# Up-products of a gated MLP with the activations stationary instead of the weights, in three parts of the hidden width

## The chip, the cores and the metric

The kernel runs on one core of one Trainium2 chip. The metric is the time of one execution on the device in microseconds (us); the median of several runs is given, and one further execution was recorded by the hardware profiler. The engines are named as the profile names them: PE is TensorE's matrix multiplication and PEld its loading of the stationary operand, DVE is VectorE, ACT is ScalarE, POOL is GpSimd, and SP issues the transfers.

## The reference

Two encoder layers work on 256 tokens of width 2048, in float32. Layer 0 mixes tokens with a bidirectional mLSTM, layer 1 with a bidirectional HGRN2 recurrence; each mixer is followed by a gated MLP with a convolution of width 3 over the tokens, and a final RMSNorm closes the trunk. The change touches the MLP, whose hidden width is 5504 (43 tiles of 128, called f tiles):

```python
def conv_glu(hn, w_up, conv_w, conv_b, w_down):
    u = hn @ w_up
    a, v = jnp.split(u, 2, axis=-1)
    s = a.shape[1]
    pad = CONV_W // 2
    ap = jnp.pad(a, ((0, 0), (pad, pad), (0, 0)))
    c = conv_b
    for j in range(CONV_W):
        c = c + ap[:, j:j + s] * conv_w[j]
    return (jax.nn.gelu(c, approximate=False) * v) @ w_down
...
    for layer in range(DEPTH):
        ...
        h = h + mix
        h = h + conv_glu(rmsnorm(h, norm_ffn_g[layer]), ffn_w_up[layer], ffn_conv_w[layer],
                         ffn_conv_b[layer], ffn_w_down[layer])
    return rmsnorm(h, final_g)
```

## The kernel before

**Precision.** Every large product is made from three products of rounded numbers. A float32 operand is split into a high part, rounded to the matmul's format (wh of a weight, xh of an activation), and the remainder (wl, xl). The product is xh wh + xh wl + xl wh. The activations xt (after a norm) and g (after the gate) are kept as 16 or 22 tiles of 128 rows by 512 columns: 256 tokens of the high part, then 256 of the remainder. The tokens are the columns, so these tiles are feature-major.

**The stream of weights.** The whole program is one list of chunks, worked off by `stream` (L152). A chunk is a set of output columns and all its k tiles (128 rows of the weight). `split_weights` (L122) loads weights in pieces of 2048 columns into one of three `raw` buffers, has ScalarE round 1024 columns at a time to `wh` (L147) and VectorE subtract to `wl` (L148); there are four buffers of each, and three such pieces are prepared ahead. PE uses them in order.

**Two kinds of chunk.** In an "fm" chunk (L199 to L209), the weights are stationary: for each k and each of two output tiles of 128 features, wh is loaded and x streamed with its 512 columns (both halves at once, L202), then wl is loaded and the 256 columns of xh are streamed (L209). The result is feature-major; its two halves lie side by side in a PSUM bank and are added by `fm_sum` (L217). In a "tm" chunk (L188 to L198), the activations are stationary: for each k and each of the two token halves, three matmuls with 512 columns of weights as the moving operand (L192 to L194). The result is token-major, 128 tokens by 512 features in one PSUM bank. A chunk of either kind uses two of four PSUM banks; the four others serve transposes and small products (`aux`).

**Side work.** `Side` holds generators for work that accompanies the stream. After each k the stream advances a clock (`side.tick`), and a generator whose time has come makes its next step. `norm.turn` (L269), for example, transposes hm by PE with the identity matrix as moving operand (L276) to build the next xt. The order of the instructions on each engine is finally set by the scheduler of the kernel language from its own estimate of when they are ready.

**The MLP** (`ffn`, L809). The hidden width is worked off in two parts, of 22 and 21 f tiles. For each f tile one fm chunk makes a and v; `done_up` (L820) adds their halves, multiplies by the norm's scale R (a row over the tokens), convolves along the tokens (L829 to L831), applies Gelu (L832), multiplies by v (L833) and splits the result into a tile g (L835, L836). After a part follow four tm chunks of down-products (`project`, L372): each multiplies the part's g tiles by 512 columns of w_down, and VectorE adds the result to hm (L378), which holds the residual in token-major form. In the second part `norm.add` then starts the next norm's squares and transposes. In the last layer the next norm is `FinalNorm`, whose `begin` loads final_g, and whose `half` ends the kernel.

A dummy transpose (`turns`, L206) stands in some fm chunks, one of them at the beginning of each second part.

Of the kernel before, what the change touches and what calls it, by code (L numbers as in the profile page):

```python
# [15 lines left out]
P = 128  # L16
# [3 lines left out]
FT = 5504 // P  # L20
FA = 22
FB = FT - FA
AH = 8
# [32 lines left out]
def trunk_kernel(ctx, tc, xT, x_d, fg_d, pp_d, cst_d, w_first, w_aq, w_ak, w_av, w_ao, w_aout,  # L56
                 w_bq, w_bv, w_bg, w_bout, w_up, w_down, out, mscr):
    nc = tc.nc
# [4 lines left out]
    ev = ctx.enter_context(tc.tile_pool(name="ev", bufs=1))  # L63
    psm = ctx.enter_context(tc.tile_pool(name="psm", bufs=4, space=PSUM))
    psa = ctx.enter_context(tc.tile_pool(name="psa", bufs=4, space=PSUM))

# [10 lines left out]
    def col(name, i):  # L77
        o = OFF[name] + i
        return pp[:, o:o + 1]

    def aux(name):
        return psa.tile([P, 512], F32, tag="aux", name=name)


    class Side:
        def __init__(self):
            self.now, self.jobs = 0.0, []

        def push(self, gen):
            self.jobs.append([gen, self.now])  # L90

# [18 lines left out]
        def drain(self):  # L110
            self.until(lambda: not self.jobs)

# [3 lines left out]
    class Chunk:  # L116
        def __init__(self, kind, src, nk, x, done, before=None, last=False, turns=0):
            self.last, self.turns = last, turns
            self.kind, self.src, self.nk, self.x, self.done, self.before = kind, src, nk, x, done, before
            self.width = {"fm": 256, "tm": 512, "first": 512 + P}[kind]  # L120

    def split_weights(chunks):  # L122

        first = True
        for ch in chunks:
            total = ch.nk * ch.width
            cuts = [0]
            if first:
                cuts = [k * ch.width for k in FIRST]
            while cuts[-1] < total:  # L130
                cuts.append(min(total, cuts[-1] + 2048))
            step = ch.width if first else 1024
            for b0, b1 in zip(cuts, cuts[1:]):
                n = b1 - b0
                raw = wpool.tile([P, 2048], F32, tag="raw", bufs=RAW, name="raw")
                nc.sync.dma_start(raw[:, :n], ch.src[:, b0:b0 + n])
                if first:
                    k0, k1 = b0 // ch.width, b1 // ch.width
                    (nc.scalar if k0 < 2 else nc.sync).dma_start(hx[:, k0:k1], xT[:, k0:k1])
                    if k0 == 0:  # L140
                        nc.scalar.dma_start(pp[:, 0:KT], pp_d[:, 0:KT])
                for c0 in range(0, n, step):
                    m = min(step, n - c0)
                    wh = wpool.tile([P, 1024], F32R, tag="wh", bufs=WB, name="wh")
                    wl = wpool.tile([P, 1024], F32R, tag="wl", bufs=WB, name="wl")
                    r = raw[:, c0:c0 + m]
                    act.copy(wh[:, :m], r)  # L147
                    dve.tensor_tensor(wl[:, :m], r, wh[:, :m].bitcast(F32), ALU.subtract)  # L148
                    yield wh, wl, m // ch.width
            first = False  # L150

    def stream(chunks):  # L152
        pieces = split_weights(chunks)
# [9 lines left out]
        for ch in chunks:  # L163
            if ch.before:
                ch.before()
            ps = [psm.tile([P, 512], F32, tag="mm", name="mm") for _ in range(3 if ch.kind == "first" else 2)]
            k = 0
# [45 lines left out]
    def split(dst, src, gcol):  # L213
        act.activation(dst[:, 0:T], src, AF.Copy, scale=gcol)  # L214
        dve.scalar_tensor_tensor(dst[:, T:2 * T], src, gcol, dst[:, 0:T].bitcast(F32), ALU.mult, ALU.subtract)

    def fm_sum(ps, dst):  # L217
# [15 lines left out]
    class Norm:  # L233

        def __init__(self, gname, goff):
            self.g, self.o = gname, goff
            self.xs, self.done = [None] * KT, False

        def take(self, k, src):
# [20 lines left out]
        def add(self, c):  # L260

            if c == 0:
                self.ss = ev.tile([P, 2, 4], F32, tag="ss8", bufs=2, name="ss8")
            cs = slice(512 * c, 512 * c + 512)
            for t in range(2):
                square(hm[:, t, cs], self.ss[:, t, c:c + 1])
            side.push(self.turn(c))

        def turn(self, c):  # L269
            yield 2.5  # L270
            for k0 in (4 * c, 4 * c + 2):
                pz = aux("pz")
                for k in (k0, k0 + 1):
                    for t in range(2):
                        o = (k - k0) * T + t * P
                        pe.transpose(pz[:, o:o + P], hm[:, t, k * P:(k + 1) * P], ident)  # L276
                for k in (k0, k0 + 1):
                    self.take(k, pz[:, (k - k0) * T:(k - k0 + 1) * T])
                yield 1.0
# [31 lines left out]
        def x(self, k):  # L311
            side.until(lambda: self.xs[k] is not None)
            return self.xs[k]

    class FinalNorm:
# [75 lines left out]

    def mlstm(norm, nxt):
        YT = [None] * KT
# [203 lines left out]
        def end():  # L597
            side.drain()
            stack.close()

        tail = project(lambda c: w_aout[c], KT, yx, nxt)
# [3 lines left out]

    def hgrn(norm, nxt):
        YT = [None] * KT
# [192 lines left out]
        def end():  # L800
            side.drain()
            stack.close()

        tail = project(lambda c: w_bout[c], KT, yx, nxt)
# [4 lines left out]
    def ffn(layer, norm, nxt):  # L809
        stack = ExitStack()  # L810
        box = {}
        chunks = []

        def begin():
            box["mp"] = stack.enter_context(tc.tile_pool(name="ff", bufs=1))
            box["mp"].tile([P, LEAD], F32, name="lead")
            if isinstance(nxt, FinalNorm):
                nxt.begin(box["mp"])

        def done_up(f, i, GT):  # L820
            def go(ps):
                mp, R = box["mp"], norm.R
# [5 lines left out]
                cw = [col("conv_w", (layer * 3 + w) * FT + f) for w in range(3)]  # L828
                dve.tensor_scalar(c, a, cw[1], col("conv_b", layer * FT + f), ALU.mult, ALU.add)  # L829
                dve.scalar_tensor_tensor(c[:, 1:T], a[:, 0:T - 1], cw[0], c[:, 1:T], ALU.mult, ALU.add)  # L830
                dve.scalar_tensor_tensor(c[:, 0:T - 1], a[:, 1:T], cw[2], c[:, 0:T - 1], ALU.mult, ALU.add)  # L831
                act.activation(c, c, AF.Gelu)  # L832
                dve.tensor_tensor(c, c, v, ALU.mult)  # L833
                g = slot(i, "g", mp)
                act.copy(g[:, 0:T], c)  # L835
                dve.tensor_tensor(g[:, T:2 * T], c, g[:, 0:T].bitcast(F32), ALU.subtract)  # L836
                GT.append(g)
            return go

        for part, (f0, nf) in enumerate(((0, FA), (FA, FB))):  # L840
            GT = []
            for i in range(nf):
                chunks.append(Chunk("fm", w_up[layer, f0 + i], KT, norm.x, done_up(f0 + i, i, GT),
                                    begin if f0 + i == 0 else None,
                                    turns=1 if part and i == 0 else 0))
            chunks += project(lambda c: w_down[layer, c][:, f0 * 512:(f0 + nf) * 512], nf,
                              lambda k, GT=GT: GT[k], nxt if part else None)
        return chunks, stack.close

# [6 lines left out]
    for _ in range(8):  # L856
        pe.matmul(idle[:, 0:P], ones[:, 0:P], ones[:, 0:P], start=True, stop=True)
    n0, n1, n2, n3 = Norm("mix_g", 0), Norm("ffn_g", 0), Norm("mix_g", KT), Norm("ffn_g", KT)
    nf = FinalNorm()
    chunks = mlstm(n0, n1)  # L860
    c, close0 = ffn(0, n1, n2)
    chunks += c
    c = hgrn(n2, n3)
    b = c[0].before

# [4 lines left out]
    chunks += c  # L870
    c, close1 = ffn(1, n3, nf)
    chunks += c
    stream(chunks)
# [3 lines left out]
def _cols(w, width):  # L877

    K, N = w.shape
    v = w.reshape(K // P, P, N // width, width).transpose(2, 1, 0, 3)  # L880
    return np.ascontiguousarray(v).reshape(N // width, P, (K // P) * width)


# [17 lines left out]
def layout(x, norm_mix_g, norm_ffn_g, mlstm_w_in, mlstm_b_gate, mlstm_head_g, mlstm_w_out, hgrn_w_in, hgrn_lb,  # L901
# [8 lines left out]
    up = A(ffn_w_up).reshape(2, KT, P, 2, FT, P).transpose(0, 4, 2, 1, 3, 5)  # L910
    qfb = np.stack([wb[:, o:o + 2048].reshape(D, BH, P) for o in (0, 6144, 8192)], axis=2).reshape(D, 3 * 2048)
# [16 lines left out]
        w_bout=_cols(A(hgrn_w_out)[0], 512),  # L928
        w_up=np.ascontiguousarray(up).reshape(2, FT, P, KT * 256),
        w_down=np.stack([_cols(A(ffn_w_down)[i], 512) for i in range(2)]),  # L930
    )


def build(nc, ins, out_shape=(2, P, D), **kw):
# [4 lines left out]
    with tile.TileContext(nc, schedule_with_timeline_sim=True) as tc:  # L939
        with ExitStack() as ctx:  # L940
            trunk_kernel(ctx, tc, ap["xT"], ap["x"], ap["fg"], ap["pp"], ap["cst"], ap["w_first"],
                         ap["w_aq"], ap["w_ak"], ap["w_av"],
                         ap["w_ao"], ap["w_aout"], ap["w_bq"], ap["w_bv"], ap["w_bg"],
                         ap["w_bout"], ap["w_up"], ap["w_down"], out, mscr, **kw)

# [11 lines left out]
```

## Time and profile before

| | |
|---|---|
| median of 3 runs | 2436.88 us (2436.76 to 2436.89) |
| span of the profiled execution | 2434.7 us |
| instructions | 36201 |
| mean granted TensorE clock | 0.998 |
| read from memory | 447.35 MB, 185 GB/s over the span |

The stages of the profiled execution, from the first matmul of each to the first of the next: mLSTM with its output product, from the start to 400.65 us; the MLP of layer 0 to 1120.57; HGRN2 with its output product to 1708.57; the MLP of layer 1 to the end. The layers' MLPs are alike to a few hundredths of a microsecond up to the last down-product.

A row of a group reads: line of the code, engine, operation, tiles as output<-inputs, shapes, xcount, then the busy time in us, the mean duration of one in ns, and the idle time of the engine before them with what ended it. A row of a window reads: the stretch, its length, the busy time and number of instructions of each engine in turn (PE, PEld, DVE, ACT, POOL), the granted clock, the busy share of the DMA engines and GB/s. A row of the timeline reads: start, duration, engine, line, operation, tiles. A row of waits reads: engine, tile and line that waited, for what, the total in us, how often, and the longest.

### The profile page before, as it was taken

To read this page: it belongs to the slowest core of one execution; us is meant where nothing else is said; L and a number is where in the kernel's file an instruction comes from. 1 tells how busy PE (TensorE), PEld (TensorE's weight loads), DVE (VectorE), ACT (ScalarE), POOL (GpSimd) and SP (SyncE) were. 2 spreads that over 40 slices of the span, in tenths; PEclk is the share of its full clock that TensorE was granted. 3 is DMA by queue.
4 is the path that set the end of the run, shared out by engine and by line. 5 is a ranking of instruction groups with operands and counts; after the bars stand their busy time and mean duration, and the time that the engine had idled before them with its cause. 6 is when DMAs were issued, how large, how long until landed. Compare 5 with 4: busy or idle time off the path is not lost.

```text
span 2434.7 us, 36201 instructions
## 1 busy us (share of the span) xinstructions
PE 2421.4 (99%) x14319; PEld 2069.5 (85%) x14319; DVE 1691.8 (69%) x2768; ACT 1207.5 (50%) x1831; POOL 160.7 (7%) x219
## 2 busy tenths in 40 slices
PE   9999999999999999999999999999999999999998
PEld 7888888888888888888888888888888888888887
DVE  7766566777645777656888989885777754677754
ACT  6655455444434444445555555545554543444443
POOL 0100000000000000001222222220000000000000
PEclk9999999999999999999999999999999999999999
DMA  7654555555555555555445554455555555555553
GB/s 288 197 182 158 188 175 188 191 190 191 185 197 189 190 184 183 192 184 183 170 171 174 174 174 167 166 183 195 181 189 189 191 195 196 184 183 188 190 187 141
DMA packets 66202, 451.85 MB, mean 186 GB/s; under 512 B 7648, under 2 KB 8160, under 8 KB 13424
## 3 DMA queue, kind: packets, MB, share of 16 engines
q1 hardware_dynamic: 63792, 442.91, 52.6%
q0 software_dynamic: 1232, 5.31, 1.0%
q8 instruction: 112, 1.84, 0.3%
q10 hardware_dynamic: 1008, 1.32, 0.2%
q14 instruction: 58, 0.48, 0.1%
HBM read 447.35 MB, written 2.16 MB: 185 GB/s over the span
## 4 chain that ended last, share of the span: by engine, by line
PE 99%; ACT 0%; DMA 0%; issue 0%; DVE 0%; SPq 0%; POOLq 0%; POOL 0%
PE mm L202 36%; PE mm L209 18%; PE mm L192 13%; PE mm L194 13%; PE mm L193 13%; PE pn L508 1%; PE pd L694 1%; PE py L742 1%; PE pz L276 0%; PE pa L694 0%; PE S L494 0%; DMA raw<-in_w_first 0%; PE pz L763 0%; ACT xt L214 0%; PE pa L719 0%
## 5 line engine op out<-in xcount | busy, mean ns | idle before, releaser
L148 DVE TENSOR_TENSOR wl<-raw,wh 128x1024 fp32r<-128x1024 f32 (+1 forms) x848 | 1031.7, 1218 | 593.1 <-ACT wh L147 584.5
L202 PE MATMUL mm<-xt,wh 128*128 128x512 f32 x3776 | 1325.2, 396 | 0.0
L147 ACT CAST wh<-raw 128x1024 fp32r<-128x1024 f32 (+1 forms) x848 | 881.1, 1041 | 877.5 <-PE mm L194 406.0
L209 PE MATMUL mm<-xt,wl 128*128 128x256 f32 x3776 | 1057.5, 280 | 0.0
L202 PEld LDWEIGHTS mm<-xt,wh 128*128 128x128 f32 x3776 | 708.4, 188 | 165.7
L209 PEld LDWEIGHTS mm<-xt,wl 128*128 128x128 f32 x3776 | 711.7, 188 | 2.2
L194 PE MATMUL mm<-wh,g 128*128 128x512 f32 x674 | 262.8, 390 | 0.0
L192 PE MATMUL mm<-wh,g 128*128 128x512 f32 x674 | 262.6, 390 | 0.0
L193 PE MATMUL mm<-wl,g 128*128 128x512 f32 x674 | 262.3, 389 | 0.0
L192 PE MATMUL mm<-wh,xt 128*128 128x512 f32 x512 | 201.1, 396 | 2.9 <-ACT xt L214 2.2
L193 PE MATMUL mm<-wl,xt 128*128 128x512 f32 x512 | 200.6, 392 | 0.4 <-DVE wl L148 0.4
L194 PE MATMUL mm<-wh,xt 128*128 128x512 f32 x512 | 200.1, 392 | 0.0
L219 ACT COPY b<-mm 128x256 f32<-128x256 f32 x237 | 87.6, 370 | 172.5 <-PE mm L209 172.5
L194 PEld LDWEIGHTS mm<-wh,g 128*128 128x128 f32 x674 | 126.5, 188 | 26.5
L193 PEld LDWEIGHTS mm<-wl,g 128*128 128x128 f32 x674 | 126.5, 188 | 26.3
L192 PEld LDWEIGHTS mm<-wh,g 128*128 128x128 f32 x674 | 126.5, 188 | 26.0
L192 PEld LDWEIGHTS mm<-wh,xt 128*128 128x128 f32 x512 | 95.6, 188 | 23.4 <-ACT xt L214 2.9
L193 PEld LDWEIGHTS mm<-wl,xt 128*128 128x128 f32 x512 | 96.5, 188 | 19.9 <-DVE wl L148 0.8
L194 PEld LDWEIGHTS mm<-wh,xt 128*128 128x128 f32 x512 | 96.3, 188 | 19.6
L220 DVE TENSOR_TENSOR a<-mm,b 128x256 f32<-128x256 f32 x86 | 36.5, 424 | 54.2 <-ACT b L219 54.2
L686 DVE COPY kq<-QK 128x256 f32<-128x256 f32 x224 | 70.1, 335 | 0.0
L712 POOL TENSOR_TENSOR G<-G 128x384 f32<-128x384 f32 (+2 forms) x96 | 67.8, 706 | 6.3
(204 smaller groups left out, 1822.3 us busy)
## 6 DMA issues: line engine op xcount, KB each, us to landing
raw<-in_w_up SPq DMA_DIRECT2D x172, 1024.0 KB, 4.8
raw<-in_w_down SPq DMA_DIRECT2D x80, 1024.0 KB, 4.7
raw<-in_w_bq SPq DMA_DIRECT2D x48, 1024.0 KB, 4.9
raw<-in_w_ao SPq DMA_DIRECT2D x16, 1024.0 KB, 4.8
raw<-in_w_aout SPq DMA_DIRECT2D x16, 1024.0 KB, 4.7
raw<-in_w_bv SPq DMA_DIRECT2D x16, 1024.0 KB, 4.7
raw<-in_w_bg SPq DMA_DIRECT2D x16, 1024.0 KB, 4.8
raw<-in_w_bout SPq DMA_DIRECT2D x16, 1024.0 KB, 4.8
```

Of the source, the lines that this page charges most:

```text
L147: act.copy(wh[:, :m], r)
L148: dve.tensor_tensor(wl[:, :m], r, wh[:, :m].bitcast(F32), ALU.subtract)
L192: pe.matmul(ps[t], xh, wh[:, c], start=st, stop=False)
L193: pe.matmul(ps[t], xh, wl[:, c], start=False, stop=False)
L194: pe.matmul(ps[t], xl, wh[:, c], start=False, stop=sp)
L202: pe.matmul(ps[f], wh[:, c:c + P], x, start=st, stop=False)
L209: pe.matmul(ps[f][:, 0:T], wl[:, c:c + P], x[:, 0:T], start=False, stop=sp)
L219: act.copy(b, ps[:, T:2 * T])
L220: dve.tensor_tensor(dst, ps[:, 0:T], b, ALU.add)
L508: pe.matmul(pn[:, 0:258], w, v, start=(i == 0), stop=(i == len(parts) - 1))
L686: dve.tensor_copy(m[:, j].rearrange("k (m p j) -> k m p j", p=2, j=h), blocks(z, h, 0, T))
L712: pool.tensor_tensor(G2, G[:, 0:6 * n:2], G[:, 1:6 * n:2], ALU.mult)
```

## The change

The up-products are made by a new kind of chunk, `Pair`, and with the other factor stationary:

- Four f tiles form a group (`GROUP = 4`). Its chunk has 512 columns of a and 512 of v. For each k tile there are four products, (token half, a or v), each of three matmuls with 512 moving columns, into four PSUM banks. The last two k tiles are worked off together, product by product, so that the banks are finished one after the other. There are three parts of 16, 16 and 11 f tiles, so ten full groups and one of three f tiles (384 columns) in each layer.
- ScalarE evicts the four banks, scaled by the norm's factor per token (a column now), to a token-major tile `at` (128 x 2 x 1024).
- For each f tile, as side work during the next chunk, PE transposes four blocks of `at` (a and v, two token halves) into one PSUM bank `pt`. ScalarE makes the middle term of the convolution from it with the bias (Identity); the two neighbours, Gelu, the product with v and the split follow as before, with v read from `pt`.
- The down-products are Pair chunks too, 1024 columns at a time, in three parts; the last 1024 columns of the very last part stay two tm chunks, which have weights of their own (`w_last`).
- All gated tiles find room in the permanent pool, since a part has at most 16. The memory of the MLP is opened earlier, at the second output product of the mixer before it, and FinalNorm's `begin` moves to the first down-product of the last part.
- PSUM is one pool of eight named banks, four in turn for the stream and four in turn for the side work.
- The dummy transposes at the beginning of the second parts are gone.

`Pair` can also use plans with the letter "S", in which seven products of sums replace eight. The plans of this change hold only "N" (two k tiles) and "H" (one), so those branches, and the helpers `forms`, `form` and `combine`, are not run.

The core of the diff:

```diff
-FA = 22
-FB = FT - FA
+PARTS = ((0, 16), (16, 16), (32, 11))
+GROUP = 4
+UP_PLAN = "NNNNNNNN"
+DOWN_PLAN = {16: "NNNNNNNN", 11: "NNNNNH"}
...
+    def split_pair(ch):
+        w, b0 = ch.w, 0
+        for kind in ch.plan:
+            n = (2 if kind == "H" else 4) * w
+            raw = wpool.tile([P, 2048], F32, tag="raw", bufs=RAW, name="raw")
+            nc.sync.dma_start(raw[:, :n], ch.src[:, b0:b0 + n])
+            b0 += n
+            if kind != "S":
+                for c0 in range(0, n, 2 * w):
+                    yield halves(raw[:, c0:c0 + 2 * w], 2 * w)
+                continue
...
+    def stream_pair(ch, take):
+        w = ch.w
+        acc = {n: main.next(n) for n in ("c11", "c12", "c22", "c21")}
+        begun = set()
+
+        def product(name, x, wt, sp=False):
+            (xh, xl), (wh, wl) = x, wt
+            for i, (a, b) in enumerate(((xh, wh), (xh, wl), (xl, wh))):
+                pe.matmul(acc[name][:, 0:w], a, b, start=name not in begun, stop=sp and i == 2)
+                begun.add(name)
...
+            n = 1 if kind == "H" else 2
+            us = [take() for _ in range(n)] if end else [None] * n
+            D = ch.form(c) if left else None
+            groups = [[i for i in range(n)]] if end else [[i] for i in range(n)]
+            for g in groups:
+                for i in g:
+                    if not end:
+                        us[i] = take()
+                for name, t, b in (("c11", 0, 1), ("c12", 0, 0), ("c22", 1, 0), ("c21", 1, 1)):
+                    for i in g:
+                        x = tok(k + i, t)
...
+                        product(name, x, part(us[i], b), end and i == g[-1])
+                    side.tick(0.68 * len(g))
+            k += n
+        ch.done(acc)
...
-                a = mp.tile([P, T], F32, tag="a", bufs=2, name="a")
-                v = mp.tile([P, T], F32, tag="v", bufs=2, name="v")
-                c = mp.tile([P, T], F32, tag="c", bufs=2, name="c")
-                fm_scaled(ps[0], R, a)
-                fm_scaled(ps[1], R, v)
...
-                dve.tensor_scalar(c, a, cw[1], col("conv_b", layer * FT + f), ALU.mult, ALU.add)
...
+                pt = aux("pt")
+                for n in range(2):
+                    for t in range(2):
+                        o = n * T + t * P
+                        pe.transpose(pt[:, o:o + P], at[:, t, n * 512 + j * P:n * 512 + (j + 1) * P], ident)
...
+                act.activation(c, pt[:, 0:T], AF.Identity, scale=cw[1], bias=col("conv_b", layer * FT + f))
+                dve.scalar_tensor_tensor(c[:, 1:T], pt[:, 0:T - 1], cw[0], c[:, 1:T], ALU.mult, ALU.add)
+                dve.scalar_tensor_tensor(c[:, 0:T - 1], pt[:, 1:T], cw[2], c[:, 0:T - 1], ALU.mult, ALU.add)
                 act.activation(c, c, AF.Gelu)
-                dve.tensor_tensor(c, c, v, ALU.mult)
+                dve.tensor_tensor(c, c, pt[:, T:2 * T], ALU.mult)
...
+                def done(acc, st=st):
+                    w = st["w"]
+                    if "at" not in st:
+                        room(st)
+                        for n, t, b in (("c11", 0, 0), ("c12", 0, 1), ("c22", 1, 1), ("c21", 1, 0)):
+                            act.activation(st["at"][:, t, 512 * b:512 * b + w], acc[n][:, 0:w], AF.Copy, scale=norm.rc[:, t:t + 1])
...
+                ch = Pair(w_up[layer, (f0 + i) // GROUP], UP_PLAN, norm.x, norm.form, lambda acc, done=done, st=st: (done(acc), side.push(raise_up(st))),
+                          middle, w=w)
...
+                def done(acc, c=c, part=part):
+                    for n, t, b in (("c11", 0, c), ("c12", 0, c + 1), ("c22", 1, c + 1), ("c21", 1, c)):
+                        h = hm[:, t, 512 * b:512 * b + 512]
+                        dve.tensor_tensor(h, h, acc[n], ALU.add)
+                    if part == len(PARTS) - 1:
+                        nxt.add(c)
+                        nxt.add(c + 1)
```

`room` waits until the f tiles of the group before have all been raised, then takes the one `at` tile; `raise_up` is the generator of the transposes and what follows them, with a pause of 3.5 of the side clock after each f tile.

More of the change, by code (lines that the diff above doesn't have):

```diff
@@ L79, in col, with __init__, next, bank @@
         return pp[:, o:o + 1]
+    class Turns:
+        def __init__(self, banks):
+            self.banks, self.i = banks, 0
+        def next(self, name):
+            self.i += 1
+            return bank(self.banks[self.i % len(self.banks)], name)
+    def bank(i, name):
+        return psum.tile([P, 512], F32, tag=f"bank{i}", name=name)
+    main, spare = Turns((0, 1, 2, 3)), Turns((4, 5, 6, 7))
     def aux(name):
-        return psa.tile([P, 512], F32, tag="aux", name=name)
+        return spare.next(name)
     class Side:
@@ L110, in drain @@
         def drain(self):
-            self.until(lambda: not self.jobs)
+            self.until(lambda: all(job[2] for job in self.jobs))
     side = Side()
@@ L125, in split_weights @@
         for ch in chunks:
+            if ch.kind == "pair":
+                yield from split_pair(ch)
+                continue
             total = ch.nk * ch.width
@@ L165, in stream, with take @@
                 ch.before()
-            ps = [psm.tile([P, 512], F32, tag="mm", name="mm") for _ in range(3 if ch.kind == "first" else 2)]
+            if ch.kind == "pair":
+                def take():
+                    fetch()
+                    return ready.pop(0)
+                stream_pair(ch, take)
+                continue
+            ps = [main.next("mm") for _ in range(3 if ch.kind == "first" else 2)]
             k = 0
@@ L389, in slot, with mlstm @@
         return where.tile([P, 2 * T], F32R, tag=f"yt{j}", name=f"{name}{j}")
-    def mlstm(norm, nxt):
+    def mlstm(norm, nxt, after):
         YT = [None] * KT
@@ L603, in mlstm, with hgrn @@
         return chunks + tail
-    def hgrn(norm, nxt):
+    def hgrn(norm, nxt, after):
         YT = [None] * KT
@@ L812, in ffn @@
         chunks = []
+        last = isinstance(nxt, FinalNorm)
         def begin():
@@ L832, in go @@
                 act.activation(c, c, AF.Gelu)
-                dve.tensor_tensor(c, c, v, ALU.mult)
-                g = slot(i, "g", mp)
+                dve.tensor_tensor(c, c, pt[:, T:2 * T], ALU.mult)
+                g = slot(i, "g")
                 act.copy(g[:, 0:T], c)
                 dve.tensor_tensor(g[:, T:2 * T], c, g[:, 0:T].bitcast(F32), ALU.subtract)
[L837 to L847, printed above, removed]
@@ new lines, in room, with combine @@
+        def room(st):
+            side.until(lambda: all("over" in o for o in st["wait"]))
+            st["at"] = box["mp"].tile([P, 2, 1024], F32, tag="at", bufs=1, name="at")
+        def combine(acc, at, w):
+            v5 = box["mp"].tile([P, 512], F32, tag="fe", bufs=1, name="v5")[:, 0:w]
+            s1, u4, u3, u = (at[:, t, 512 * b:512 * b + w] for t in range(2) for b in range(2))
+            act.copy(s1, acc["m1"][:, 0:w])
+            act.copy(v5, acc["c22"][:, 0:w])
+            dve.tensor_tensor(u, s1, acc["m6"][:, 0:w], ALU.add)
+            dve.tensor_tensor(u3, u, acc["m7"][:, 0:w], ALU.add)
+            dve.tensor_tensor(u4, u, v5, ALU.add)
+            dve.tensor_tensor(u, u3, v5, ALU.add)
@@ L909, in layout @@
         bg[r:r + AH, 0] = A(mlstm_b_gate)[0, i * AH:(i + 1) * AH]
-    up = A(ffn_w_up).reshape(2, KT, P, 2, FT, P).transpose(0, 4, 2, 1, 3, 5)
+    up = A(ffn_w_up).reshape(2, KT, P, 2, FT, P)[:, :, :, ::-1].transpose(0, 2, 1, 3, 4, 5)
+    groups = np.zeros((2, FT // GROUP + 1, P, KT * 2 * GROUP * P), np.float32)
+    for i in range(0, FT, GROUP):
+        v = up[:, :, :, :, i:i + GROUP].reshape(2, P, -1)
+        groups[:, i // GROUP, :, :v.shape[2]] = v
     qfb = np.stack([wb[:, o:o + 2048].reshape(D, BH, P) for o in (0, 6144, 8192)], axis=2).reshape(D, 3 * 2048)
```

235 lines of the change are left out of this document (207 added, 28 removed).

## The prediction

> **What bounds the kernel now.** I read the page from the top: busy shares and clock, then the chain that ended last, and then the waits of TensorE's queue.
>
> ```profile
> span 2434.7 us, 36201 instructions
> PE 2421.4 (99%) x14319; PEld 2069.5 (85%) x14319; DVE 1691.8 (69%) x2768; ACT 1207.5 (50%) x1831; POOL 160.7 (7%) x219
> PEclk9999999999999999999999999999999999999999
> PE 99%; ACT 0%; DMA 0%; issue 0%; DVE 0%; SPq 0%; POOLq 0%; POOL 0%
> ```
> ```profile
> PE mm L192 <- ACT xt L214: 2.2, 2, 2.0
> PE idle L857 <- POOL ones L851: 1.1, 1, 1.1
> PE mm L192 <- ACT wh L147: 0.7, 1, 0.7
> PE mm L193 <- DVE wl L148: 0.4, 1, 0.4
> ```
>
> The chain is 99% PE, the clock is full in every slice, and PE waited 4.4 us in all. So the time is the number of PE instructions times what each takes up in the queue. VectorE has 31% to spare and ScalarE half. The profiled execution spans 2434.7 us and the median of the runs is 2436.88; I make the sum on the span and add the 2.2 us between them at the end.
>
> What an instruction takes up is not its row's duration, because matmuls overlap. These rows give durations (mean ns after the comma), by which a 512-column matmul would cost 396 or 390 ns:
>
> ```profile
> L202 PE MATMUL mm<-xt,wh 128*128 128x512 f32 x3776 | 1325.2, 396 | 0.0
> L209 PE MATMUL mm<-xt,wl 128*128 128x256 f32 x3776 | 1057.5, 280 | 0.0
> L194 PE MATMUL mm<-wh,g 128*128 128x512 f32 x674 | 262.8, 390 | 0.0
> ```
>
> The cost is read from whole stages of layer 0: up-products, down-products, up, down (window, its length, PE busy and count; PEclk stands before the DMA share):
>
> ```profile
> 400.65:646.17 245.52, 245.52 (x1421) 214.83 (x1420) 178.85 (x289) 123.93 (x183) 0.69 (x1) 1.00 0.56 190
> 646.17:765.88 119.71, 119.71 (x530) 99.11 (x529) 60.90 (x60) 47.53 (x48) 0.00 (x0) 1.00 0.54 192
> 765.88:1003.41 237.53, 237.53 (x1347) 206.02 (x1345) 168.07 (x266) 114.05 (x165) 0.00 (x0) 1.00 0.55 187
> 1003.41:1120.57 117.16, 117.16 (x531) 96.81 (x530) 62.55 (x71) 54.39 (x72) 0.00 (x0) 1.00 0.53 183
> ```
>
> (Counts hold neighbours at the edges; the code gives 22 x 64 = 1408 matmuls in the first up stage, 22 x 24 = 528 in the first down stage, 21 x 64 = 1344 and 21 x 24 = 504 in the others.) The first down stage has nothing but 512-column matmuls with activations stationary: 119.71 / 528 = 226.7 ns each. The second up stage has one small extra instruction: 237.53 / 1344 x 2 = 353.5 ns for one 128x128 weight tile (512 columns through wh and 256 through wl). The first up stage also holds 12 small PE instructions:
>
> ```profile
> L276 PE MATMUL pz<-cst,hx 128*128 128x128 f32 x8 | 1.4, 272 | 0.0
> L296 PE MATMUL pr<-dg,ones 128*128 128x128 f32 x4 | 0.6, 273 | 0.0
> ```
>
> **The transposes' price.** The second down stage holds the 24 transposes of the next norm:
>
> ```profile
> L276 PE MATMUL pz<-cst,hx 128*128 128x128 f32 x24 | 4.1, 272 | 0.0
> ```
>
> Its matmuls alone are 504 x 0.2267 = 114.3 us; the stage takes 117.16, so 24 transposes cost 2.9 us, 120 ns each. The rows around them show how it goes (start, duration):
>
> ```profile
> 1037.95 0.39 PE L193 MATMUL mm<-wl,g 128*128 128x512 f32 x1
> 1038.18 0.82 PE L276 MATMUL pz<-cst,hx 128*128 128x128 f32 x6
> 1038.76 0.48 PE L194 MATMUL mm<-wh,g 128*128 128x512 f32 x1
> 1039.07 0.40 PE L192 MATMUL mm<-wh,g 128*128 128x512 f32 x1
> ```
>
> Between 1037.95 and 1039.07 lie two matmuls (0.453) and six transposes: 0.667 us, 111 ns each. I take 120, which holds what the matmuls behind them lose too, and 111 as the lower bound. The upper bound is the duration, 272. With 12 x 0.12 = 1.4 us taken off, the first up stage is 244.1 / 704 = 346.7 ns a weight tile.
>
> The Trainium skill (TensorE: Matmul & The Clock Gate, Part 4: PE-mode transpose) gives about 275 ns for a transpose in a kernel and says that transposes don't count as work for the clock gate. The duration agrees (272), but the stage was lengthened by 120 each, and its granted clock stayed 1.00. By that figure the transposes below would cost 94.6 us.
>
> **The change, part by part.** *Up-products.* Removed per layer: 244.1 + 237.4 = 481.5 us of weights-stationary matmuls. Added per layer: ten groups of four f tiles and one of three (4+4+4+4, 4+4+4+4, 4+4+3). A full group is 16 k x 4 products x 3 matmuls = 192 matmuls of 512 columns, 192 x 0.2267 = 43.5 us; ten make 435.3. The last group has 192 of 384 columns, for which no row exists. Bounds: three quarters of 226.7 (170) and all of it. The 256-column step of the first up stage takes 346.7 - 226.7 = 120; a straight line from it to 226.7 gives 173 for 384 columns: 33.2 us, at most 43.5. Sum 468.5; saved 13.0 a layer, **26.0 us** in both. As many columns flow as before; what is saved is the overhead of the short wl matmul.
>
> *Transposes.* Each f tile now needs four (a and v, two token halves): 43 x 2 x 4 = 344. At 120 ns that is **41.3 us** (38.2 at 111, 93.6 at 272). Nothing hides it: PE is the bound and each transpose is a PE instruction.
>
> *Down-products.* 43 x 24 matmuls a layer as before, same shape, in three parts instead of two: 0 on PE. The additions into hm are made three times rather than twice, 8 more a layer at 0.68 us, on VectorE only.
>
> *Evictions.* Per f tile ScalarE drops two copies (L219) and VectorE two additions and two products with R (L220, L225), and L829 goes to ScalarE. New are four scaled evictions of 128x512 per group on ScalarE; the nearest row is the mixer's:
>
> ```profile
> L575 ACT ACTIVATE sg<-mm,rc 128x512 f32<-128x512 f32 x8 | 5.3, 680 | 0.0
> L378 DVE TENSOR_TENSOR hx<-hx,mm 128x512 f32<-128x512 f32 x46 | 30.0, 681 | 8.5 <-PE mm L194 8.5
> L147 ACT CAST wh<-raw 128x1024 fp32r<-128x1024 f32 x824 | 865.0, 1051 | 857.2 <-PE mm L194 388.2 <-issue 241.4 <-PE mm L202 206.3
> L148 DVE TENSOR_TENSOR wl<-raw,wh 128x1024 fp32r<-128x1024 f32 x824 | 1013.5, 1231 | 576.1 <-ACT wh L147 567.4
> L831 DVE SCALAR_TENSOR_TENSOR c<-a,pp,c 128x255 f32<-128x255 f32 x86 | 41.0, 477 | 0.0
> L833 DVE TENSOR_TENSOR c<-c,v 128x256 f32<-128x256 f32 x86 | 35.9, 417 | 1.0 <-ACT c L832 1.0
> L832 ACT ACTIVATE c<-c 128x256 f32<-128x256 f32 x86 | 36.0, 419 | 23.3 <-DVE c L831 23.3
> L835 ACT CAST g<-c 128x256 fp32r<-128x256 f32 x86 | 34.4, 400 | 0.0
> L832 ACT ACT_TABLE_LOAD x2 | 2.6, 1283 | 0.0
> ```
>
> ScalarE in a group of 45 us: 16 casts (16.8), 4 evictions (2.7), 4 x (0.42 + 0.42 + 0.40) = 5.0: 24.5 us. VectorE: 16 x 1.23 + 4 x (0.48 + 0.48 + 0.42 + 0.42) = 26.9 us. Both are covered by PE. Identity with a bias is not in the trace; if it shared no table with Gelu, two loads of 1.28 us per f tile would bring ScalarE to 35 of 45 us, still covered. Cost 0 for all of this, as long as the hand-over below holds.
>
> *Weights.* A piece of 1024 columns now lasts 12 x 0.2267 = 2.72 us of PE, before 8 x 0.347 = 2.77; the 1.05 us cast and the 1.23 us subtraction still fit. At a group's end two pieces are held to the last matmul, so the cast into the first one's buffer comes 2 us late; two further pieces, 5.4 us of PE, are ready by then. The first down pair asks for the last group's gated tiles only at k = 12 (33 us on), or at k = 8 in the part of eleven. Cost 0. FinalNorm's load of final_g moves past all of the last layer's up-products, into the end with 60 us of PE to cover it: 0.
>
> Sum: 2434.7 - 26.0 + 41.3 = 2450.0; with the 2.2 us of the runs, **2452**.
>
> **Rivals.** *Hand-over of PSUM (slower still).* A group fills all four main banks, where a chunk filled two of four, and the next group starts on the same four. The last bank (c21) ends with the group. If ScalarE has just begun a cast, its eviction is done 0.16 (end of the matmul row after the next start) + 1.05 + 0.68 = 1.9 us later; PE asks for that bank after nine matmuls, 2.04 us. It fits by 0.15 us. The f tile's transposes read all four evictions, and the code pushes them behind the first three matmuls (0.68 us): if PE keeps that order, it waits 1.2 us a group, 22 x 1.2 = 27 us: 2479. With two casts ahead it is 2.3 us, 50 in all: 2502. Against it: in the rows above the six transposes stand between L193 and L194 of one product, where the code has no place for them, so the order is made by readiness. The Trainium skill (Perfetto Trace Analysis, Matmuls) asks that independent groups rotate through different banks, so that evacuation overlaps; the change keeps that for three of four banks. The old down stages, which do rotate, show 226.7 ns without a gap.
>
> *Absorbed transposes (faster).* A matmul can start almost at once behind a transpose:
>
> ```profile
> 1036.34 0.39 PE L193 MATMUL mm<-wl,g 128*128 128x512 f32 x1
> 1036.57 0.27 PE L276 MATMUL pz<-cst,hx 128*128 128x128 f32 x1
> 1036.60 0.47 PE L194 MATMUL mm<-wh,g 128*128 128x512 f32 x1
> 1036.91 0.39 PE L192 MATMUL mm<-wh,g 128*128 128x512 f32 x1
> ```
>
> If a transpose cost those 0.03 us, 344 make 10.3, the kernel gains 15.7 us and ends at 2421. It decides below 26.0 / 344 = 76 ns. Against it: the matmul behind then holds the queue for 0.31 us, not 0.227, and from 1036.34 to 1036.91 a single transpose has cost 0.117 in all.
>
> *Transposes by duration.* 344 x 0.272 = 93.6, less 26.0: 2504. Against it stands the stage sum of 120. The skill's 275 ns, in the place named above, would speak for it.
>
> *The two cancel.* The two up stages show that one stream can settle at two paces, 346.7 and 353.5. The hgrn stages behind the change have 768 weight tiles (24 chunks, 16 k, two tiles each), 5.2 us from one pace to the other; with a transpose half-way between break-even and lower bound (94 ns, 32.3 us) the sum is 32.3 - 26.0 - 5.2 = +1.1: 2438.
>
> **How the numbers follow.** Sum as worked out, 2444 to 2460: 0.70. Hand-over, 2460 to 2502: 0.16. By duration: 0.02. Cancelled: 0.06, and nearly all of it within 0.2%, which is 4.9 us and about what a measurement can tell from none. Absorbed: 0.06. So slower by over 0.2%: 0.86; within: 0.08, with the forecast's own lower edge; faster: 0.06. The range runs from 2441 to 2478: below lie the absorbed and half of the cancelled, above lies the worse half of the hand-over; about 2 in 10 are left out.
>
> **What would show it.** The up stages with 512 columns: start to start 226 to 227 ns in long stretches, and a full group some 43.5 us plus 16 transposes, 45.4. 344 more transposes of 128x128 in pt. Matmul counts of the down stages unchanged. Waits of PE on the evictions or on pt's banks of more than a few us would show the hand-over; a spacing of 231 or more in the groups, or groups of 46 us and longer without waits, would make my pace wrong; groups of 44 us would show absorbed transposes.

## The result, and the profile after

| | us |
|---|---|
| before, median of 4 runs | 2436.89 (2436.76 to 2437.34) |
| after, median of 4 runs | 2494.06 (2492.68 to 2496.13) |
| ratio | 1.0234, 95% interval 1.022 to 1.0249 |
| predicted | 2452 (2441 to 2478) |
| span of the profiled execution, whose own time was 2493.22 | 2491.4 (before 2434.7) |

The change made the kernel slower, as forecast, but by 57 us instead of 15, outside the range. The page after, with the parts that answer to those shown of before:

```profile
span 2491.4 us, 33784 instructions
PE 2452.4 (98%) x13381; PEld 2059.6 (83%) x13381; DVE 1556.3 (62%) x2359; ACT 1247.0 (50%) x1838; POOL 160.3 (6%) x219
PE 93%; DVE 4%; issue 1%; ACT 1%; DMA 0%; SPq 0%; POOLq 0%; POOL 0%; DVEq 0%; ACTq 0%
```

The chain is no longer 99% PE: VectorE has 4% of it. TensorE's waits name the place (engine, tile and line, for what; total us, times, longest):

```profile
PE pa L893 <- DVE QK L882: 24.4, 7, 3.9
PE mm L326 <- ACT xt L348: 2.8, 2, 1.6
PE mm L326 <- ACT wh L173: 1.4, 1, 1.4
```

L893 is in the hgrn mixer, which the MLP's edits don't touch: the first product into `pa` waits for VectorE's last product of a head's levels (L882). No wait of PE on an eviction of a group, or on `pt`, is in the list. The windows of the four sections of the program, before (mLSTM, MLP of layer 0, hgrn, MLP of layer 1; length, then busy time and count of PE, PEld, DVE, ACT, POOL, then the granted clock):

```profile
0.00:400.65 400.65, 396.25 (x1962) 334.20 (x1962) 263.47 (x435) 221.98 (x358) 18.36 (x37) 1.00 0.58 197
400.65:1120.57 719.92, 719.92 (x3823) 616.76 (x3822) 470.38 (x685) 339.90 (x466) 0.69 (x1) 1.00 0.55 188
1120.57:1708.57 588.00, 588.00 (x4742) 504.28 (x4741) 487.08 (x962) 309.32 (x548) 139.88 (x178) 1.00 0.51 175
1708.57:2434.70 726.13, 717.22 (x3798) 614.30 (x3796) 470.89 (x689) 336.30 (x459) 1.81 (x3) 1.00 0.54 185
```

The same four sections after:

```profile
0.00:402.66 402.66, 396.95 (x1961) 334.36 (x1962) 263.45 (x435) 221.75 (x358) 17.76 (x37) 1.00 0.58 197
402.66:1129.33 726.67, 726.67 (x3346) 606.30 (x3345) 400.48 (x486) 358.73 (x465) 0.69 (x1) 1.00 0.52 187
1129.33:1757.69 628.36, 603.83 (x4749) 514.30 (x4748) 490.78 (x956) 310.35 (x552) 140.03 (x178) 0.98 0.47 163
1757.69:2491.40 733.71, 724.94 (x3329) 604.66 (x3327) 401.62 (x485) 356.16 (x463) 1.81 (x3) 1.00 0.51 183
```

The differences are +2.0, +6.8, +40.4 and +7.6 us. The two MLPs, where everything that the diff says of products and transposes takes place, cost 14.4 us more; 15.3 had been worked out. The 0.9 us between them went into hgrn: eight transposes of the norm behind the first MLP now come after its last product (hgrn's stretch up to the first head's stream has 16 of them instead of 8, and takes 35.59 us instead of 34.69). Seven tenths of the loss are in hgrn, where PE stood still for 628.36 - 603.83 = 24.5 us and was busy 15.8 us longer with the same products but for those eight.

The first of the seven waits, on PE, after (start, duration, line, tiles, count; the bracket gives the idle time before and who ended it):

```profile
1176.97 0.39 PE L328 MATMUL mm<-wh,xt 128*128 128x512 f32 x1
1177.29 0.45 PE L869 MATMUL pd<-kq 128*32 128x32 f32 x28
1181.61 0.46 PE L893 MATMUL pa<-QK 128*128 128x128 f32 x2 [3.88 <-DVE QK L882]
...
1183.01 0.91 PE L869 MATMUL pd<-kq 128*32 128x32 f32 x50
...
1184.71 0.63 PE L327 MATMUL mm<-wl,xt 128*128 128x512 f32 x1
1185.13 0.63 PE L328 MATMUL mm<-wh,xt 128*128 128x512 f32 x1
1185.56 0.60 PE L326 MATMUL mm<-wh,xt 128*128 128x512 f32 x1
1185.99 0.40 PE L327 MATMUL mm<-wl,xt 128*128 128x512 f32 x1
1186.23 0.39 PE L328 MATMUL mm<-wh,xt 128*128 128x512 f32 x1
```

And the same place before:

```profile
1171.39 0.40 PE L194 MATMUL mm<-wh,xt 128*128 128x512 f32 x1
1171.63 0.39 PE L718 MATMUL pa<-QK 128*128 128x128 f32 x2
...
1172.78 0.86 PE L694 MATMUL pd<-kq 128*32 128x32 f32 x78
```

Two things are to be seen. First, the order: before, pa's products come first and all of pd's follow; after, some of pd's come ahead of pa. Second, VectorE is not late. The stage's first stream matmul starts at 1155.26 before and at 1164.92 after; pa starts 16.4 us behind it in the one and 16.7 in the other. It is PE that arrives there 3.9 us early, having been given 54 of its stream's matmuls ahead of pa instead of 72 (18 x 0.227 = 4.1 us), and stands still until VectorE has finished. After the wait the stream's matmuls start 0.42 to 0.43 us apart, not 0.227, until 1186. The granted clock in windows around it (before the wait, in it, and twice after it; the value behind POOL's):

```profile
1164.92:1177.70 12.78, 12.78 (x84) 10.28 (x82) 12.78 (x27) 6.80 (x11) 6.44 (x6) 1.00 0.49 165
1177.70:1181.60 3.90, 0.04 (x3) 0.02 (x1) 3.90 (x9) 0.00 (x0) 2.98 (x5) 1.00 0.63 204
1181.60:1185.00 3.40, 3.39 (x90) 3.00 (x91) 3.37 (x10) 0.80 (x2) 0.00 (x0) 0.65 0.40 111
1185.00:1194.66 9.66, 9.66 (x42) 7.85 (x41) 8.73 (x24) 4.45 (x8) 0.00 (x0) 0.95 0.44 150
```

So this wait is paid twice: once as idle time, and again as slower work behind it. Over all of hgrn the trace has the clock at half for 27.3 us, in six stretches (their rows are in the last section). PE was busy in 25.9 of these, which costs it at most half, 12.9 of the 15.8 us that it was busy longer; 0.9 are the eight transposes, and the rest was not traced. The Trainium skill (TensorE: Matmul & The Clock Gate, Why this matters for your kernels) says to leave no gap of more than some 3 us on PE, or the clock falls to half; this trace agrees in the place shown, with a gap of 3.88 us and matmuls at nearly twice their spacing (0.42 to 0.43 us for 0.227).

What in the diff reaches hgrn is its PSUM: two pools of four buffers, from which any tile of `mm` or `aux` took one, became eight named banks, given out in turn as the code is traced. That these banks delay hgrn is theory A of the runs below. The rival B was that the new MLP ahead of hgrn disturbs it.

### The profile page after: what moved, and what is told of

The parts are those of the page before. It is cut to its first block, busy times and chain, and to the rows that moved or that the text cites. A ratio compares the mean times of both kernels' runs of the same rounds, so it can differ in the third digit from the quotient of the medians.

```text
span 2491.4 us, 33784 instructions
## 1 busy us (share of the span) xinstructions
PE 2452.4 (98%) x13381; PEld 2059.6 (83%) x13381; DVE 1556.3 (62%) x2359; ACT 1247.0 (50%) x1838; POOL 160.3 (6%) x219
## 3 DMA queue, kind: packets, MB, share of 16 engines
q8 instruction: 105, 1.72, 0.3%
## 4 chain that ended last, share of the span: by engine, by line
PE 93%; DVE 4%; issue 1%; ACT 1%; DMA 0%; SPq 0%; POOLq 0%; POOL 0%; DVEq 0%; ACTq 0%
PE c L215 55%; PE mm L336 9%; PE mm L326 6%; PE mm L327 6%; PE mm L328 6%; PE mm L343 5%; PE pt L1017 2%; DVE wl L174 1%; DVE QK L881 1%; DVE kq L861 1%; PE pn L682 1%; PE py L917 1%; PE pd L869 1%; PE pa L869 0%; DVE QK L882 0%
## 5 line engine op out<-in xcount | busy, mean ns | idle before, releaser
L215 PE MATMUL c<-wh,xt 128*128 128x512 f32 (+1 forms) x2816 | 876.3, 388 | 0.0
L215 PEld LDWEIGHTS c<-wh,xt 128*128 128x128 f32 x2816 | 527.3, 188 | 99.0
L215 PE MATMUL c<-wl,xt 128*128 128x512 f32 (+1 forms) x1408 | 538.3, 385 | 0.0
L215 PE MATMUL c<-wh,g 128*128 128x512 f32 x1288 | 405.1, 392 | 0.0
L336 PE MATMUL mm<-xt,wh 128*128 128x512 f32 x1024 | 362.1, 396 | 0.0
L215 PEld LDWEIGHTS c<-wl,xt 128*128 128x128 f32 x1408 | 264.7, 188 | 47.2
L343 PE MATMUL mm<-xt,wl 128*128 128x256 f32 x1024 | 289.6, 283 | 0.0
L215 PE MATMUL c<-wl,g 128*128 128x512 f32 x644 | 249.8, 390 | 0.0
L336 PEld LDWEIGHTS mm<-xt,wh 128*128 128x128 f32 x1024 | 191.9, 188 | 42.2
L343 PEld LDWEIGHTS mm<-xt,wl 128*128 128x128 f32 x1024 | 193.7, 189 | 1.7
```

The source lines that it names most:

```text
L215: pe.matmul(acc[name][:, 0:w], a, b, start=name not in begun, stop=sp and i == 2)
L336: pe.matmul(ps[f], wh[:, c:c + P], x, start=st, stop=False)
L343: pe.matmul(ps[f][:, 0:T], wl[:, c:c + P], x[:, 0:T], start=False, stop=sp)
```

## The experiments

**The banks alone, on the kernel before** (e1):

```diff
-    psm = ctx.enter_context(tc.tile_pool(name="psm", bufs=4, space=PSUM))
-    psa = ctx.enter_context(tc.tile_pool(name="psa", bufs=4, space=PSUM))
+    psum = ctx.enter_context(tc.tile_pool(name="psum", bufs=1, space=PSUM))
...
+    main, spare = Turns((0, 1, 2, 3)), Turns((4, 5, 6, 7))
     def aux(name):
-        return psa.tile([P, 512], F32, tag="aux", name=name)
+        return spare.next(name)
```

> The kernel before, with one edit: its two PSUM pools (four buffers each) become the eight named banks of the change, four in turn for the stream and four in turn for the side work. Nothing of the MLP is changed. Theory A (the named banks alter the order in which TensorE is given the hgrn stage's small products, so that it waits for VectorE there): hgrn with its output product grows from 588 to about 628 us, mLSTM by 2, the MLPs stay at 720; in all 2437 + 42 = 2479. Rival B (the new MLP before it is what delays hgrn): no change, 2437 within 3 us.

Measured: 2479.62 us (2474.16 to 2480.18), ratio 1.0171 (1.0155 to 1.0186). Its waits and its hgrn section:

```profile
PE pa L730 <- DVE QK L719: 23.8, 7, 3.6
```
```profile
1120.45:1752.24 631.79, 607.83 (x4741) 517.50 (x4740) 490.75 (x962) 309.57 (x548) 139.67 (x178) 0.97 0.47 163
```

With not one line of the MLP changed, the same wait appears and hgrn is 43.8 us longer. Theory A holds; the 2 us in mLSTM do not come from it (400.53 here).

**The pools put back into the changed kernel**, for everything (e2), for the side work alone (e3), for the stream alone (e4):

```diff
     def aux(name):
-        return spare.next(name)
+        return psa.tile([P, 512], F32, tag="aux", name=name)
```

> The changed kernel with the two PSUM pools of the kernel before in place of the eight named banks; the up-products stay token-major. Theory A: the hgrn stage goes back to 588 us and only the MLP's sum is left, 2494 - 42 = 2452. Rival B: 2494, hgrn at 628. Rival C (the pools also disturb the pairs, which take all four buffers at once): hgrn 588, but the MLPs longer than 727 and 734 us, above 2460.

> The changed kernel, with the pool of four buffers for the side work alone; the stream keeps its four named banks. Theory A1 (the side work's banks are what counts, since pa and pd are side work): 2452, hgrn at 588. Rival A2 (the stream's banks count): 2494, hgrn at 628.

> The changed kernel, with the pool of four buffers for the stream alone; the side work keeps its four named banks. Theory A1: no change, 2494 and hgrn at 628. Rival A2: 2452 and hgrn at 588.

Measured: e2 2453.37 us, ratio to before 1.007 (1.0053 to 1.0086); e3 2453.08, ratio 1.0067 (1.0052 to 1.0082); e4 2493.86 in one run, its hgrn at 630.5. Of the diff's two sets of banks it is the side work's that cost the time. The MLPs take 726.7 and 733.7 us in all three, so the pools do not disturb the pairs (rival C). Of e3, hgrn and the wait:

```profile
1128.14:1717.76 589.62, 589.41 (x4749) 505.38 (x4748) 487.53 (x956) 310.04 (x552) 140.17 (x178) 1.00 0.50 174
```
```profile
PE pa L894 <- DVE QK L883: 0.2, 1, 0.2
```

PE's busy time in hgrn is back too, 589.41 against 603.83, and the clock is 1.00: nearly all of the longer busy time went with the waits.

**The order alone** (e5): the changed kernel keeps its named banks, but pd's products are held behind pa's in TensorE's order.

```diff
-            pe.matmul(pa[:, 3 * P:4 * P], KZ[:, T + P:2 * T], QZ[:, 0:P], start=True, stop=True)
+            tail = pe.matmul(pa[:, 3 * P:4 * P], KZ[:, T + P:2 * T], QZ[:, 0:P], start=True, stop=True)
...
+            with tc.issue_after(tail.ins):
+                for i in reversed(range(FINE)):
+                    product(pd[:, (i + 1) * 64:(i + 2) * 64], *ms[i], QUAD)
+                product(pd[:, 0:64], ks, q, QUAD)
```

> The changed kernel with its named banks, and one edge of order: a head's products into pd come behind its two products into pa (L893, L894) in TensorE's order, as they stand in the code and as the kernel before issues them. Nothing is computed otherwise. Theory A: the wait comes from the fourteen pd products that are issued ahead of pa, because pd has a bank of its own and its inputs are ready sooner, and that bring pa forward with them, 18 stream matmuls too early; then the waits of pa on VectorE fall from 24 us to below 2, hgrn takes 588 and the kernel 2453. Rival D (the banks delay VectorE or the release of a bank itself): 2494 remains, or most of it.

Measured: 2454.55 us, ratio to before 1.007 (1.0054 to 1.0087). The place of the first wait:

```profile
1181.12 0.39 PE L328 MATMUL mm<-wh,xt 128*128 128x512 f32 x1
1181.72 0.46 PE L893 MATMUL pa<-QK 128*128 128x128 f32 x2 [0.21 <-DVE QK L882]
...
1182.95 0.86 PE L869 MATMUL pd<-kq 128*32 128x32 f32 x78
```

pa comes 16.7 us behind the start of the stage's stream again, with the stream running up to it. The banks as such cost hgrn nothing (589.7 us here, 589.6 in e3); the early start of pd that goes with them does. That the named banks let pd start early is read from these orders. How they do it, and why the planner then places pa right behind those products, before its input can be there, was not looked into.

**The price of a transpose** (e6): on e3, each transpose into `pt` is issued twice.

```diff
-                        pe.transpose(pt[:, o:o + P], at[:, t, n * 512 + j * P:n * 512 + (j + 1) * P], ident)
+                        for _ in range(2):
+                            pe.transpose(pt[:, o:o + P], at[:, t, n * 512 + j * P:n * 512 + (j + 1) * P], ident)
```

> The changed kernel with the pool for the side work (2453.1) and each transpose into pt issued twice, one behind the other, into the same place: 344 more PE instructions, nothing else. Theory: a transpose takes 120 ns of TensorE's queue, so 2453 + 41 = 2494. Rival (back to back they cost only their spacing): 109 to 111 ns, 2491. Rival (their duration): 272 ns, 2547. Rival (absorbed): below 10 us, 2463 or less.

Measured: 2489.68 us, 36.6 more than e3: 36.6 / 344 = 106 ns. The stages say the same: the first up stage took 186.48 us with 48 more transposes, 181.38 in e3, and the first down stage 90.70 with 16 more, 89.00 in e3, in both 106 ns each. It is the rival's value, a little under: an added transpose behind another costs its spacing, and the 120 ns hold in addition what the return to the stream costs. The duration of 272 ns and the absorbed transpose are both out.

**The two paces of the old up stages.** The prediction worked with 346.7 and 353.5 ns a weight tile for the same stream. A kernel in which the second stages ran like the first would beat the one before. No dummy transpose there (e7), two (e8), one hitch in the order (e9, which runs the branch of the next diff for the first k tile alone):

```diff
-                                    turns=1 if part and i == 0 else 0))
+                                    turns=0 if part and i == 0 else 0))
```

> The kernel before without the dummy transpose at the beginning of each second up stage. The second up stages run at 353.5 ns a weight tile, the first ones at 346.7 after twelve small instructions. Theory (the pace is a matter of where a small instruction last shifted the stream): with none there the second stages either keep 353.5 (2436.9) or fall to 346.7 (2 x 672 x 6.8 ns = 9.1 less: 2427.7). Rival (part two is slower for another reason, its data or its buffers): 2436.7 and 353.5.

> The kernel before with two dummy transposes instead of one at the beginning of each second up stage. If the pace is a matter of where a small instruction last shifted the stream, one of none and two may fall to 346.7 ns a weight tile: 2427.9. Otherwise 353.5 and 2437.1.

> The kernel before, with the first k tile of each second up stage issued as two 512-column matmuls and then two 256-column ones, in place of the dummy transpose; all the rest alternates as before. In the first up stages the pace goes from 353 to 347 ns a weight tile behind such a hitch at 413.2 us, and none and two dummy transposes did not move it. Theory (the pace is set by the last hitch in the alternation and then kept): the second up stages run at 346.7, 2 x 672 x 6.8 ns = 9.1 us less, 2427.7. Rival (such a hitch has nothing to do with it): 2436.7.

Measured: e7 2436.76 and e8 2437.26 us in one run each, e9 2436.65, ratio 1.0001 (0.9992 to 1.001). The second up stage of e7 takes 237.44 us, 353.3 ns a tile. All three expectations of a gain missed: none, one or two dummy transposes and this hitch at the stage's beginning leave the pace where it is. What sets it stays open, but the premise of e9 does not hold. In the first up stage of before, a weight tile took 350, 350 and 361 ns in turn (some 353.5 on average) up to 409.28 us, and 346 or 347 from 410.77 on. The change lies behind four small products at 409.51 us (L296) and ahead of the hitch at 413.2; behind four transposes at 405.89 us the pace had stayed. So a group of small products can move the pace, and no run here says when it does.

**Another order of the old up-products** (e10, e11): two 512-column matmuls, then two 256-column ones, in all up stages or in the second ones alone.

```diff
+                        if ch.turns == 9:
+                            cs = [kk * ch.width + f * P for f in range(2)]
+                            for f in range(2):
+                                pe.matmul(ps[f], wh[:, cs[f]:cs[f] + P], x, start=st, stop=False)
+                            side.tick(0.325 * len(ps))
+                            for f in range(2):
+                                pe.matmul(ps[f][:, 0:T], wl[:, cs[f]:cs[f] + P], x[:, 0:T], start=False, stop=sp)
```

> The kernel before, with every k tile of the MLP's up-products issued as two 512-column matmuls and then two 256-column ones. Theory (a 512-column matmul takes 227 behind another one, and a 256-column one 113 to 117): 340 to 344 ns a weight tile in all four up stages; against 346.7 and 353.5 that is 704 x 3 to 7 + 672 x 10 to 13 ns a layer, in both 17 to 28 us less, 2409 to 2420. Rival (the 256-column ones behind each other wait for their weights, 188 ns by their rows): longer than 2437, up to 2437 + 2752 x 0.07 = 2630.

Measured: 2432.02 us, ratio 0.9982 (0.9973 to 0.999): faster, but by 4.6 us and not by 17 to 28: a weight tile takes 348.3 ns and not 340 to 344. Its first and second up stage:

```profile
401.30:647.86 246.56, 246.56 (x1421) 215.21 (x1420) 177.03 (x289) 121.56 (x182) 0.69 (x1) 1.00 0.56 189
767.57:1001.64 234.07, 234.07 (x1346) 204.24 (x1344) 166.22 (x266) 111.56 (x164) 0.00 (x0) 1.00 0.56 190
```

Both now run at one pace, (246.56 - 1.4) / 704 and 234.07 / 672 = 348.3 ns: the slow stage gains, the fast one loses a little.

> The kernel before, with the paired order (two 512-column matmuls, then two 256-column ones) in the second up stage of each layer alone; the first up stages keep the alternation, in which they run at 346.7 ns a weight tile. With the paired order in all four the second stages took some 234.0 us instead of 237.5, the first ones 246.4 instead of 245.5. Expected: 2 x 3.5 us less than before, 2429.6. Rival (the hgrn stages behind it fall into another order and take it back): 2432 or more.

Measured: 2430.17 us (2430.07 to 2430.26), ratio 0.9971 (0.996 to 0.9982), as expected. It is the fastest kernel of the study, and beats both: the weights stay stationary, and only the second up stages issue in pairs.

## Why the prediction was wrong, point by point

**The up-products: right.** 26.0 us were to be saved. After, the first up stage, the first down stage and the third up stage with the short group are:

```profile
402.66:584.03 181.37, 181.37 (x829) 149.87 (x828) 98.44 (x123) 94.06 (x125) 0.69 (x1) 1.00 0.51 186
584.03:673.04 89.01, 89.01 (x402) 73.55 (x400) 49.38 (x55) 38.39 (x46) 0.00 (x0) 1.00 0.53 189
942.01:1066.13 124.12, 124.12 (x609) 108.50 (x608) 66.58 (x81) 62.28 (x84) 0.00 (x0) 1.00 0.52 183
```

The first holds 768 stream matmuls and 60 small instructions, 48 of them in `pt` (the fourth group is raised in the next stage): 768 x 0.2267 = 174.1 leaves 7.3 us, 121 ns each. The second holds 384 and 16 transposes: 87.05 leaves 1.96, 122 ns each. The third has 384 long ones (87.05), 32 transposes (3.9) and 192 of 384 columns: 33.2 us, 173 ns each, the value of the straight line.

**The transposes: right** at 120 ns; nothing hid them. The rival by which the two cancel is out as well: with the waits gone (e3), hgrn took 1.6 us more than before and not 5.2 less. The clock did not mind them either: it stands at 1.00 in all these windows.

**Evictions, weights, down-products at 0: right.** The list of waits has none of them: its wait for wh is 16.6 us from the start, in the mLSTM mixer. The new eviction and the Identity took 688 and 563 ns on ScalarE (680 and 420 had been put down), and Gelu's table was loaded once in that stage:

```profile
L1081 ACT ACTIVATE at<-c,rc 128x512 f32<-128x512 f32 x15 | 10.3, 688 | 6.6 <-PE c L215 6.6
L1019 ACT ACTIVATE c<-pt,pp 128x256 f32<-128x256 f32 x12 | 6.8, 563 | 12.7 <-PE pt L1017 12.7
L1022 ACT ACT_TABLE_LOAD x1 | 1.3, 1283 | 0.0
```

**The hand-over of PSUM within the MLP: did not happen**, though its range, 2460 to 2502, holds the measured time. That is chance: the price was paid in another stage and by another mechanism.

**The step that failed** is the list of parts itself. It costed the edits of the MLP and let hgrn move by "5.2 us from one pace to the other" and no more. The diff's edit of `aux`, which serves every stage, got no term. With it taken back the kernel takes 2453.1 us, 1 us from the 2452 of the sum; with it alone the old kernel loses 42.9 us. What the runs put in the missing term's place: named banks let pd's first products go ahead of pa's, pa comes forward with them, PE waits seven times some 3.5 us for VectorE, and the clock falls behind most of these waits.

**Open**: mLSTM ended 2.0 us later. It ended between 400.5 and 403.0 us in all kernels of this study, whichever banks they had. Of the 2.0 us, 1.3 are longer waits in the first 17 us (xt and wh, 4.2 us together instead of 2.9); the rest wasn't followed up.

## What to carry to other kernels

An edit of a shared helper, a pool or an allocator belongs to every stage that draws from it: go through all its callers, and give each a term or a bound, also where no instruction changes. Where a planner sets the order of an in-order queue, more freedom for one product can pull a waiting one to the front; compare the order of the queue before and after, stage by stage, not the instruction counts. On a queue that is the bound, take prices from whole stages, not from the rows' durations: here this gave the part that had been thought of to within 1 us.

## What the runs showed of the hardware that had not been expected

A wait of little more than 3 us halves TensorE's clock, but not each time and not for a fixed time. The seven waits of the changed kernel lasted 3.88, 3.29, 3.47, 3.28, 3.62, 3.28 and 3.61 us. Its trace holds six stretches at half clock behind them (PE's busy time and count, then the clock; the windows are cut a little inside):

```profile
1182.59:1186.00 3.41, 3.41 (x85) 0.50 0.46 115
1247.45:1254.26 6.81, 6.03 (x95) 0.50 0.65 236
1383.98:1387.38 3.40, 3.40 (x68) 0.50 0.60 171
1452.25:1455.65 3.40, 3.40 (x33) 0.50 0.76 255
1517.10:1520.50 3.40, 3.10 (x86) 0.50 0.41 137
1585.37:1592.18 6.81, 6.51 (x53) 0.50 0.46 155
```

They last 3.41 or 6.83 us, and over 400 us all their bounds lie on one grid with steps of 3.413 us, wherever the waits fall. Each begins at the end of a step in which PE had stood idle for 1.9 us or more; for the wait of 3.28 us at 1379 it was 1.93 us. The third wait, of 3.47 us, was split between two steps, 1.77 and 1.70 us idle, and the clock stayed full:

```profile
1312.30:1315.71 3.41, 1.64 (x57) 1.00 0.88 305
1315.71:1319.12 3.41, 1.71 (x64) 1.00 0.01 2
```

In e4 a wait split into 1.74 and 1.72 us was followed by a stretch at half clock, so in these runs the limit lies near 1.75 us of idle time in a step, and no sharper than that. In e1 the stretches in hgrn add up to 41.0 us, half of which is 20.5, and PE was busy 19.8 us longer there. The Trainium skill (TensorE: Matmul & The Clock Gate, Part 1) has a free-running window of 3.4 us, by which a wait's place in the window would decide; the trace agrees, with its grid of 3.413 us and the third wait.

The other surprise is the alternating stream of 512 and 256 columns, which settles at about 347 or 353.5 ns a weight tile and keeps its pace for over 200 us, while pairs of each run at 348.3. The stream of 512 columns alone ran at 226.7 ns again between its transposes, in the second down stage before and in the up stages after.
